# Feed-forward half of an encoder block: weight blocks of the next quarter prepared inside the present one, seven products in a new order, squares on ScalarE

## The chip, the core and the metric

The program runs on one core of a Trainium2 chip. Five engines work side by side, each through its own list of instructions in a fixed order: TensorE (PE; its weight loads are PEld) multiplies matrices and writes PSUM banks, VectorE (DVE) and ScalarE (ACT) do elementwise work, GpSimd (POOL) does a little of it, and SyncE (SP) issues most of the transfers. An instruction that waits holds up everything behind it on its own engine. The metric is the device time of one execution in microseconds (us). The kernel before takes 742.55 us (median of three runs, 742.44 to 743.73).

## The reference, cut to what matters

One encoder layer on 512 rows of 1024 columns, in float32. The change lies in the second half, and in the weights that are loaded for it:

```python
x = layer_norm(DEEPNORM_ALPHA * x + mix, ln1_g[l], ln1_b[l])         # x: 512 x 1024
h = jnp.square(jax.nn.relu(jnp.einsum("bsd,df->bsf", x, w_ff1[l])))   # w_ff1: 1024 x 4096
ff = jnp.einsum("bsf,fd->bsd", h, w_ff2[l])                          # w_ff2: 4096 x 1024
x = layer_norm(DEEPNORM_ALPHA * x + ff, ln2_g[l], ln2_b[l])
```

`mix` comes from two attention branches, two branch products with sigmoid gates, and an output product.

## The kernel before, in words

**Precision.** Every float32 operand is split into a high part h, rounded by a copy on ACT (L84), and a low part l = source - h, made on DVE (L85). A product is three matmuls: h*h, h*l and l*h (L184 to L186 where the weights are stationary, L189 to L191 where the activations are). A *split* below is this pair, one instruction on ACT and one on DVE.

**The feed-forward half in four quarters.** Each quarter takes 1024 of the 4096 hidden columns. Its first part is four *column pairs* (`t_pair`): each multiplies all 1024 rows of `w_ff1` for two blocks of 128 hidden columns, 8 steps of 3 matmuls for each of two banks, 48 matmuls; four pairs are 192. The two results of a pair go to the functions `first(i)` and `second(i)`: ReLU on ACT (L896), the square on DVE (L897), and then sums, differences and splits. These are the left operands of Strassen's scheme in Winograd's form: the quarter's second product, a 2 by 2 block product, is done with **seven products** instead of eight. Their left operands are A11, A12, A22 and the sums S1 to S4 of blocks of h; their right operands are four blocks of `w_ff2` (b11, b12, b22, b21 for each i from 0 to 3) and sums of these. Product n is 2 banks by 4 values of i by 3 matmuls: 24 matmuls, and seven are 168. `prepare(n, i)` makes the right operand of product n for block i: the subtractions that it needs (L866) and a split. `run(n, ...)` issues product n's matmuls. Before, the order is 1, 6, 2, 7, 5, 4, 3; A11, S2 and S3 are the left operands of 1, 6 and 7.

**Where the weights come from.** SP loads `w_ff1` as 512 KB chunks (`raw`, L126), which are split into `wh` and `wl` ahead of their use, and `w_ff2` as 256 KB blocks (L927). Before, a quarter's sixteen blocks lie in the tiles called X; they are loaded and split while the quarter's own column pairs run and while its products run.

**Results.** A product's two banks are added into U (`u`) and into the residual rows x1 (`x`) on DVE (L853, L855, L1018, L1025); only then is the bank free for the next product but one. Two pairs of banks, W and Z, collect products 7 and 5 over all four quarters. In the last quarter the rows are finished one block of 128 at a time: layer norm (statistics on DVE at L863, L728; L736 and L742 apply it) and the store. The last block is cut in two halves of 256 columns that share one bank.

**What sets the order.** The order of the instructions on each engine is fixed when the program is built. A scheduler interleaves the program's text with what it takes to be ready; tiles are handed out again in the order in which they come free. The V tiles (24 of them) hold right and left operands in a round: a split into a V tile waits until the product that read its earlier content has gone by on PE.

**Before the feed-forward half** come the second branch product (L610 on DVE, L613 on POOL, L615 on ACT, L616 on DVE), and the output product in two halves of columns with four row blocks each: L719 adds, L723 to L790 do the first layer norm, and L801 turns the normalised rows on PE. The sixteen gates lie in the tiles called G, which come free one by one during the second branch product; in the feed-forward half of the kernel before, G holds A12 with A22, and S4 with S1.

Of the kernel before, what the change touches and what calls it, by code (L numbers as in the profile page):

```python
# [40 lines left out]
def block_kernel(ctx, tc, w, w2, x_t, x, pos, relb, bgate, lq1, lk1, lq2, lk2, subg,  # L41
# [773 lines left out]

    c0 = next_chunk[0] + 4
    for i in range(4):
        dest[c0 + i] = ([vt(), vt()], [vt(), vt()])
    for n, _ in enumerate(s_group(mh, ml, evac_res(0))):
        prefetch(c0 + 5, min(c0 + 4, next_chunk[0] + 3))  # L820
    fin = evac_res(1)
# [19 lines left out]

    U = [late.tile([P, S], F32, name=f"u{b}") for b in range(2)]
    touched = set()

# [8 lines left out]
    def row_stats(s, nh, lo=0, hi=S):  # L858
        width = S if s < NT - 1 else 256
# [4 lines left out]

    def sub(out, a, b):
        V.tensor_tensor(out=out, in0=a, in1=b, op=ALU.subtract)  # L866

    LEFT = {1: "A11", 2: "A12", 3: "S4", 4: "A22", 5: "S1", 6: "S2", 7: "S3"}
    lo_rows, hi_rows = slice(0, 256), slice(256, S)

    class Quarter:


        def __init__(self, q):
            self.q = q
            self.ops = {n: [None] * 4 for n in range(1, 8)}
            self.raw = [None] * 4
            self.a = {}
            a11 = self.halves(vt)
            self.ops[1] = [(vt(), vt()) for _ in range(4)]  # L880
            s2 = self.halves(vt)
            self.ops[6] = [(vt(), vt()) for _ in range(4)]
            s3 = self.halves(lambda: late.tile([P, S], FR, tag="s3", bufs=4, name=name("s3")))
            for i in range(4):
                self.a["A11", i], self.a["S2", i], self.a["S3", i] = a11[i], s2[i], s3[i]

        def halves(self, make):

            two = [(make(), make()) for _ in range(2)]
            return [tuple(t[:, 256 * j:256 * (j + 1)] for t in pair)  # L890
                    for pair in two for j in range(2)]


        def square(self, ps):
            t = tmp_tile()
            A.activation(t, ps, AF.Relu)  # L896
            V.tensor_tensor(out=t, in0=t, in1=t, op=ALU.mult)  # L897
            return t

        def first(self, i):  # L900
            def f(ps):
                t = self.t0 = self.square(ps)
                sub(t[:, hi_rows], t[:, lo_rows], t[:, hi_rows])
                split(t[:, lo_rows], *self.a["A11", i])
                split(t[:, hi_rows], *self.a["S3", i])
            return f

        def second(self, i):
            def f(ps):
                t, t0 = self.square(ps), self.t0  # L910
                s2 = tmp_tile()[:, lo_rows]
                sub(s2, t[:, hi_rows], t0[:, hi_rows])
                for left, right in (("A12", "A22"), ("S4", "S1")):
                    h, l = gt(FR), gt(FR)
                    split(t, h, l)
                    self.a[left, i] = h[:, lo_rows], l[:, lo_rows]
                    self.a[right, i] = h[:, hi_rows], l[:, hi_rows]
                    if left == "A12":
                        split(s2, *self.a["S2", i])
                        sub(t[:, lo_rows], t[:, lo_rows], s2)  # L920
                        V.tensor_tensor(out=t[:, hi_rows], in0=s2, in1=t0[:, lo_rows], op=ALU.add)
            return f


        def load(self, i, r, c, t=None):
            t = t or xt()
            nc.sync.dma_start(out=t, in_=w2[self.q, i, r, :, c * S:(c + 1) * S])  # L927
            return t

# [3 lines left out]
        def prepare(self, n, i, parts=None):  # L933
            b11, b12, b22, b21 = self.raw[i]
            src = {1: b11, 6: b22, 2: b21, 7: b12, 5: b11, 4: b22, 3: b11}[n]
            if n == 6:
                sub(b22, b22, b11)
# [221 lines left out]
```

## Time and profile before

| what | us |
|---|---|
| median of three runs (lowest, highest) | 742.55 (742.44, 743.73) |
| the profiled execution, its own time | 744.0 |
| its span from first to last instruction | 742.2 |
| PE busy | 709.8 |
| DVE busy | 546.9 |
| ACT busy | 361.9 |

The span is what the traces show; the execution's own time holds 1.8 us beside it. Times in the rows are us from the start of the span. In 40 equal slices the page gives PE nine tenths or more nearly everywhere; slices with less lie at the last fifth of the run, and DVE is at nine there in its turn.

### The profile page before, as it was taken

What the parts mean: (1) busy time and instruction counts of PE and PEld (TensorE: products, weight loads), DVE (VectorE), ACT (ScalarE), POOL (GpSimd) and SP (SyncE); (2) the same over time, 40 slices, a digit from 0 to 9 for tenths busy, and PEclk for the clock granted to TensorE, in tenths of its full rate; (3) what the DMA queues carried; (4) which work ended last, traced back from release to release, by engine and by line L of the source; (5) the groups of instructions that cost most, each with busy time, mean ns of one, the idle gap of its engine ahead of it and who ended that gap; (6) DMA issues with size and microseconds to landing.
All of it is one profiled execution on the core that took longest, in us unless ns stands there. A gap on an engine that the chain in (4) does not pass through costs nothing.

```text
span 742.2 us, 9457 instructions
## 1 busy us (share of the span) xinstructions
PE 709.8 (96%) x3259; PEld 583.1 (79%) x3259; DVE 546.9 (74%) x1046; ACT 361.9 (49%) x666; POOL 100.5 (14%) x107
## 2 busy tenths in 40 slices
PE   9999999999999999999999879999999989999991
PEld 7888888888888888888898658887688868888771
DVE  6567578765678656747779996389946798288998
ACT  5556566545567665325455461256514563155420
POOL 1022367631111210141000000000000000000001
PEclk9999999999999999999999989999999999999996
DMA  8554224232322122614272328021451308111013
GB/s 301 181 165 127 73 81 120 69 114 86 115 85 86 57 86 86 218 66 170 78 254 94 114 67 275 31 83 57 150 191 57 113 1 283 58 58 57 1 60 110
DMA packets 34511, 83.07 MB, mean 112 GB/s; under 512 B 5408, under 2 KB 6176, under 8 KB 34464
## 3 DMA queue, kind: packets, MB, share of 16 engines
q1 hardware_dynamic: 33600, 81.37, 33.4%
q10 hardware_dynamic: 864, 1.11, 0.4%
q8 instruction: 25, 0.41, 0.2%
q14 instruction: 22, 0.18, 0.1%
HBM read 75.65 MB, written 2.10 MB: 105 GB/s over the span
## 4 chain that ended last, share of the span: by engine, by line
PE 73%; DVE 20%; ACT 4%; issue 2%; DMA 1%; DVEq 0%; ACTq 0%
PE mm L184 9%; PE mm L186 9%; PE mm L185 9%; DVE V L85 5%; PE st L184 4%; PE st L185 4%; PE st L186 4%; PE mm L190 4%; PE mm L191 4%; PE mm L189 4%; DVE X L866 3%; PE st L190 2%; PE st L191 2%; PE st L189 2%; DVE G L85 1%
## 5 line engine op out<-in xcount | busy, mean ns | idle before, releaser
L85 DVE TENSOR_TENSOR wl<-raw,wh 128x1024 fp32r<-128x1024 f32 (+1 forms) x86 | 105.0, 1221 | 27.1 <-ACT wh L84 27.1
L84 ACT CAST wh<-raw 128x1024 fp32r<-128x1024 f32 (+1 forms) x86 | 88.6, 1030 | 69.1 <-PE mm L185 25.1
L184 PE MATMUL mm<-X,wh 128*128 128x512 f32 x256 | 103.2, 403 | 0.0
L186 PE MATMUL mm<-X,wl 128*128 128x512 f32 x256 | 99.9, 390 | 0.0
L185 PE MATMUL mm<-X,wh 128*128 128x512 f32 x256 | 99.8, 390 | 0.0
L84 ACT CAST V<-X 128x512 fp32r<-128x512 f32 x108 | 61.6, 618 | 40.3 <-DMA X<-in_w_dram 25.1
L186 PE MATMUL st<-x1t,wl 128*128 128x512 f32 (+1 forms) x200 | 76.1, 381 | 0.0
L185 PE MATMUL st<-x1t,wh 128*128 128x512 f32 (+1 forms) x200 | 76.1, 381 | 0.0
L184 PE MATMUL st<-x1t,wh 128*128 128x512 f32 (+1 forms) x200 | 75.9, 381 | 0.0
L85 DVE TENSOR_TENSOR V<-X,V 128x512 fp32r<-128x512 f32 x108 | 70.9, 680 | 5.0 <-ACT V L84 5.0
L186 PEld LDWEIGHTS mm<-X,wl 128*128 128x128 f32 x256 | 48.0, 188 | 10.5
L184 PEld LDWEIGHTS mm<-X,wh 128*128 128x128 f32 x256 | 48.2, 188 | 8.8
L185 PEld LDWEIGHTS mm<-X,wh 128*128 128x128 f32 x256 | 48.2, 188 | 8.6
L767 POOL TENSOR_SCALAR s<-s 128x1 f32<-128x1 f32 x1 | 0.4, 410 | 398.3 <-DVE s L751 398.3
L285 ACT ACTIVATE e<-e,s 128x128 f32<-128x128 f32 (+3 forms) x64 | 36.0, 563 | 35.4 <-DVE s L283 34.7
L378 POOL TENSOR_SCALAR e<-e,s 128x128 f32<-128x128 f32 (+3 forms) x32 | 36.8, 1149 | 66.3 <-DVE s L287 62.4
L186 PEld LDWEIGHTS st<-x1t,wl 128*128 128x128 f32 x200 | 37.6, 188 | 7.6 <-DVE wl L85 0.5
L185 PEld LDWEIGHTS st<-x1t,wh 128*128 128x128 f32 x200 | 37.6, 188 | 7.2
L184 PEld LDWEIGHTS st<-x1t,wh 128*128 128x128 f32 x200 | 37.5, 188 | 7.0
L866 DVE TENSOR_TENSOR X<-X,X 128x512 f32<-128x512 f32 x64 | 42.3, 680 | 0.1
L189 PE MATMUL mm<-wh,X 128*128 128x512 f32 x96 | 39.0, 409 | 0.7 <-ACT wh L84 0.7
L190 PE MATMUL mm<-wl,X 128*128 128x512 f32 x96 | 38.4, 400 | 0.0
(267 smaller groups left out, 1600.0 us busy)
## 6 DMA issues: line engine op xcount, KB each, us to landing
raw<-in_w_dram SPq DMA_DIRECT2D x86, 512.0 KB
X<-in_w_dram SPq DMA_DIRECT2D x80, 256.0 KB
q<-q SPq DMA_DIRECT2D x32, 128.0 KB
G<-in_relb_dram SPq DMA_DIRECT2D x8, 256.0 KB
x<-in_x_dram SPq DMA_DIRECT2D x4, 512.0 KB
e<-in_x_t_dram SPq DMA_DIRECT2D x7, 256.0 KB
raw<-in_w_dram SPq DMA_DIRECT2D x4, 256.0 KB
out_dram<-x SPq DMA_DIRECT2D x3, 256.0 KB
```

The source lines that it names most:

```text
L84: A.copy(out=h, in_=src)
L85: i = (eng or V).tensor_tensor(out=l, in0=src, in1=h.bitcast(F32), op=ALU.subtract)
L184: T.matmul(ps, lw_h, rh, start=first, stop=False)
L185: T.matmul(ps, lw_h, rl, start=False, stop=False)
L186: T.matmul(ps, lw_l, rh, start=False, stop=last)
L189: T.matmul(ps, ah, w_h, start=first, stop=False)
L190: T.matmul(ps, ah, w_l, start=False, stop=False)
L191: T.matmul(ps, al, w_h, start=False, stop=last)
L285: A.activation(e[:, :n], e[:, :n], AF.Exp, bias=nm, scale=-1.0, accum_out=sums)
L378: G.tensor_scalar(ex[:, :n], ex[:, :n], r, None, op0=ALU.mult)
L767: G.tensor_scalar(nmr, mv[:, 0:1], -1.0, None, op0=ALU.mult)
L866: V.tensor_tensor(out=out, in0=a, in1=b, op=ALU.subtract)
```

## The change

Five things, all in the feed-forward half and just ahead of it.

1. The class `Quarter` loads its sixteen blocks of `w_ff2` when it is made, into G tiles in place of X tiles, and it is made during the **quarter before** (ahead of product 4); the first one during the first half of the output product. The three sums of the right operands are a function of their own, `sums(i)`, and with product 7's operand they are made then too.
2. The products run in the order **7, 5, 1, 6, 2, 4, 3**; product 5's operand is prepared within the column pairs, the others one product ahead.
3. Two blocks are loaded a second time, since sums overwrite them (in `prepare`, at n = 7 and n = 5; before, one block).
4. The square moves from DVE to ACT.
5. In the last quarter, the residual rows are finished in the order 2, 0, 3, 1 with products 4, 2 and 3 for each block; the last block is row block 1 (`LAST_ROW`), where it was 3. Operands A12/A22 and S4/S2 lie in X tiles, S3 and S1 in V tiles, A11 in a pool of its own.

```diff
+        def __init__(self, q):
...
+            self.raw = [[self.load(i, r, c) for r, c in ((0, 0), (0, 1), (1, 1), (1, 0))]
+                        for i in range(4)]
+            self.ops[7] = [(vt(), vt()) for _ in range(4)]
...
         def square(self, ps):
             t = tmp_tile()
             A.activation(t, ps, AF.Relu)
-            V.tensor_tensor(out=t, in0=t, in1=t, op=ALU.mult)
+            A.activation(t, t, AF.Square)
             return t
...
+        def sums(self, i):
+            b11, b12, b22, b21 = self.raw[i]
+            sub(b11, b12, b11)
+            sub(b12, b22, b12)
+            sub(b22, b22, b11)
...
+            src = {1: b12, 2: b21, 3: b11, 4: b22, 5: b11, 6: b22, 7: b12}[n]
             self.ops[n][i] = self.ops[n][i] or parts or (vt(), vt())
             split(src, *self.ops[n][i])
-            if n == 1:
-                sub(b11, b12, b11)
-                sub(b12, b22, b12)
+            if n == 7:
+                self.load(i, 0, 0, b12)
             if n == 5:
                 self.load(i, 1, 1, b11)
+            if n == 6:
+                sub(b22, b21, b22)
...
     for n, _ in enumerate(s_group(mh, ml, evac_res(0))):
         prefetch(c0 + 5, min(c0 + 4, next_chunk[0] + 3))
+        if n == 0:
+            qt = Quarter(0)
+        if n in (2, 4):
+            for i in (n - 2, n - 1):
+                qt.sums(i)
+                qt.prepare(7, i)
...
     for q in range(4):
-        qt, last = Quarter(q), q == 3
+        last = q == 3
+        qt.left_tiles()
+        qt.ops[5] = [(vt(), vt()) for _ in range(4)]
...
-            for n, k in ((), ((1, 0),), ((1, 1), (6, 0)), ((1, 2), (1, 3), (6, 1)))[i]:
-                qt.prepare(n, k)
+            prepare(5, (i,))
...
+        qt.run(7, W, **ends)
+        prepare(1)
...
+        qt.run(5, Z, **ends)
+        prepare(6)
...
+        prepare(2)
         X = bank_pair()
         qt.run(1, X)
-        prepare(6, (2, 3))
...
+        prepare(4)
         X = bank_pair()
         qt.run(6, X)
-        prepare(7)
...
         if not last:
-            qt.run(7, W, **ends)
-            prepare(4)
-            qt.run(5, Z, **ends)
             prepare(3)
+            X = bank_pair()
+            qt.run(2, X)
+            following = Quarter(q + 1)
+            for b in range(2):
+                add_to(b, 0, X[b])
+            for i in range(4):
+                following.sums(i)
+                following.prepare(7, i)
             X = bank_pair()
             qt.run(4, X)
...
         for b in range(2):
+            X, Y, X2 = ([mm_bank()] * 2 for _ in range(3))
...
+            qt.run(4, X, (b,))
...
+            qt.run(2, Y, (b,))
...
+            for lo, hi in ((0, 256), (256, S)) if b == LAST_ROW else ((0, S),):
+                qt.run(3, X2, (b,), cuts=((lo, hi),))
+                add_to(b, 1, X2[b][:, lo:hi], lo, hi)
+                row_stats(b, 1, lo, hi)
+            (layer_norm_last if b == LAST_ROW else layer_norm)(b, *lnc, store_row(b))
```

PE, early in the second quarter's products, the kernel before: product 6 for both row blocks (banks o_5099 and st_5100), with its waits; the first name behind the arrow is the weight part, the second the left operand.

```order
2328 L191 MATMUL st_5100<-V_4637,V_4634 128x512
2329 L189 MATMUL o_5099<-V_4639,V_4633 128x512 [waits Activation_49]
2330 L189 MATMUL st_5100<-V_4639,V_4633 128x512
2331 L190 MATMUL o_5099<-V_4640,V_4633 128x512 [waits DVE_49]
2332 L191 MATMUL o_5099<-V_4639,V_4634 128x512
2333 L189 MATMUL o_5099<-V_4641,V_4635 128x512 [waits Activation_49]
2334 L190 MATMUL st_5100<-V_4640,V_4633 128x512
```

The same engine and quarter, the kernel after: the second product that runs is now 5, into bank mm_4341 and then mm_4342.

```order
2329 L189 MATMUL mm_4341<-V_4705,V_4695 128x512
2330 L190 MATMUL mm_4341<-V_4706,V_4695 128x512
2331 L191 MATMUL mm_4341<-V_4705,V_4696 128x512
2332 L189 MATMUL mm_4341<-V_4707,V_4695 128x512 [waits Activation_49]
2333 L190 MATMUL mm_4341<-V_4708,V_4695 128x512
2334 L191 MATMUL mm_4341<-V_4707,V_4696 128x512 [waits DVE_49]
2335 L189 MATMUL mm_4342<-V_4701,V_4693 128x512
```

Before, each i of the second product waits for ACT and for DVE to prepare its weights. After, the only wait there is for the fourth block's left operand S1 (V_4695 and V_4696).

DVE in the second quarter's products, the kernel before, at the splits for products 2, 7 and 5 (V from X) between additions into u and x.

```order
746 L85 TENSOR_TENSOR V_5084<-X_4655,V_5083 128x512 [waits Activation_49]
747 L1025 TENSOR_TENSOR u_3817<-u_3817,o_5099 128x512 [waits PE_49]
748 L85 TENSOR_TENSOR V_5088<-X_4742,V_5087 128x512 [waits Activation_49]
749 L1025 TENSOR_TENSOR u_3818<-u_3818,st_5100 128x512 [waits DVE_49,PE_49]
750 L85 TENSOR_TENSOR V_5092<-X_4750,V_5091 128x512 [waits Activation_49]
```

The kernel after at the matching place: splits for product 6, its subtractions, and subtractions for the third quarter's blocks (G_5277 to G_5281).

```order
730 L85 TENSOR_TENSOR V_5131<-G_4571,V_5130 128x512 [waits Activation_49]
731 L823 TENSOR_TENSOR G_5277<-G_5279,G_5277 128x512 [waits DMAHW3_49,DMAHW2_49]
732 L823 TENSOR_TENSOR G_4571<-G_4573,G_4571 128x512 [waits DMAHW1_49,DVE_49]
733 L85 TENSOR_TENSOR V_5136<-G_4579,V_5135 128x512 [waits PE_49,Activation_49]
734 L823 TENSOR_TENSOR G_5279<-G_5281,G_5279 128x512 [waits DMAHW4_49,DVE_49]
735 L823 TENSOR_TENSOR G_4579<-G_4581,G_4579 128x512 [waits DVE_49]
736 L85 TENSOR_TENSOR V_5141<-G_4587,V_5140 128x512 [waits Activation_49]
737 L823 TENSOR_TENSOR G_5281<-G_5281,G_5277 128x512 [waits DVE_49]
```

DVE now waits there for transfers of the next quarter (DMAHW) and, through ACT, for PE to free V tiles.

DVE in the second branch product, the difference between the two kernels (+ is new): G_3459 to G_3471 are blocks of the first quarter's `w_ff2`.

```order
+L823 TENSOR_TENSOR G_3459<-G_3461,G_3459 128x512
+L823 TENSOR_TENSOR G_3461<-G_3463,G_3461 128x512
 L616 SCALAR_TENSOR_TENSOR X_3335<-G_2528,X_3334 128x512
+L823 TENSOR_TENSOR G_3463<-G_3463,G_3459 128x512
 L610 SCALAR_TENSOR_TENSOR G_2790<-G_2790,st_3338 128x512
 L85 TENSOR_TENSOR wl_3424<-raw_3357,wh_3423 128x1024
+L823 TENSOR_TENSOR G_3467<-G_3469,G_3467 128x512
 L616 SCALAR_TENSOR_TENSOR X_3354<-G_2722,X_3353 128x512
 L610 SCALAR_TENSOR_TENSOR G_2937<-G_2937,st_3363 128x512
```

Twelve such subtractions and four splits (product 7's operand) now stand in DVE's queue between the branch product's additions and the output product's first layer norm.

## Rows read from the trace of the kernel before

**Rows 1.** Who waited for whom on PE, whole span: us, times, longest

```profile
PE st L189 <- DVE x L853: 10.4, 4, 7.9
PE o L190 <- DVE V L85: 7.0, 5, 5.3
```

**Rows 2.** Busy time by stretch: us, PE, PEld, DVE, ACT, POOL (count), PEclk, DMA

```profile
418.96:468.00 49.04, 41.80 (x170) 32.38 (x168) 39.29 (x66) 19.07 (x34) 0.00 (x0) 0.93 0.46 150
511.52:553.87 42.35, 40.29 (x169) 31.05 (x168) 33.28 (x56) 16.29 (x29) 0.00 (x0) 1.00 0.44 149
597.39:639.72 42.33, 40.28 (x170) 31.08 (x168) 33.26 (x56) 16.30 (x29) 0.00 (x0) 1.00 0.44 150
683.24:733.55 50.31, 41.43 (x181) 33.00 (x179) 50.18 (x92) 15.66 (x30) 0.00 (x0) 0.93 0.17 56
...
468.00:511.52 43.52, 43.52 (x194) 36.04 (x192) 30.93 (x53) 21.06 (x36) 0.00 (x0) 1.00 0.22 73
```

**Rows 3.** PE in order of time, first quarter's products: start, us, operation, [idle before]

```profile
423.27 0.39 PE L191 MATMUL st<-V,V 128*128 128x512 f32 x1
428.97 0.80 PE L190 MATMUL o<-V,V 128*128 128x512 f32 x1 [5.31 <-DVE V L85]
...
433.52 0.39 PE L189 MATMUL st<-V,V 128*128 128x512 f32 x1
```

**Rows 4.** PE in order of time, second quarter's products

```profile
525.80 0.50 PE L189 MATMUL st<-V,G 128*128 128x512 f32 x1 [0.97 <-DVE x L853]
```

**Rows 5.** DVE groups, 468 to 553.9: count, busy us, mean ns, idle before

```profile
L866 DVE TENSOR_TENSOR X<-X,X 128x512 f32<-128x512 f32 x16 | 10.6, 680 | 0.0
...
L897 DVE TENSOR_TENSOR lt<-lt 128x512 f32<-128x512 f32 x8 | 5.5, 684 | 5.4 <-ACT lt L896 5.4
```

**Rows 6.** ACT groups, whole span

```profile
L896 ACT ACTIVATE lt<-st 128x512 f32<-128x512 f32 x24 | 14.2, 592 | 35.8 <-PE st L186 35.6
...
L527 ACT ACTIVATE e<-o 128x512 f32<-128x512 f32 x4 | 2.3, 585 | 1.0 <-PE o L524 1.0
```

**Rows 7.** DVE in order of time, 425 to 560

```profile
447.94 5.50 DVE L85 TENSOR_TENSOR V<-X,V 128x512 fp32r<-128x512 f32 x9
...
483.40 0.42 DVE L866 TENSOR_TENSOR lt<-lt,lt 128x256 f32<-128x256 f32 x1
483.73 0.42 DVE L921 TENSOR_TENSOR lt<-lt,lt 128x256 f32<-128x256 f32 x1
```

**Rows 8.** All engines in order of time, end of the last quarter

```profile
730.09 0.20 DVE L728 BATCH_NORM_AGGREGATE s<-bn 128x2 f32<-128x12 f32 x1
730.21 0.37 DVE L853 TENSOR_TENSOR x<-x,st 128x256 f32<-128x256 f32 x1
...
730.63 0.58 PE L189 MATMUL st<-V,G 128*128 128x256 f32 x1 [7.91 <-DVE x L853]
...
734.19 0.40 DVE L853 TENSOR_TENSOR x<-x,st 128x256 f32<-128x256 f32 x1
```

**Rows 9.** The chain that ended last, in order of time: start, us, what

```profile
359.71 0.87 PE mm L801 x8
...
707.55 3.13 DMA X<-in_w_dram
...
731.24 0.07 DVE s L741
731.31 0.65 DVE x L736
```

**Rows 10.** DVE in order of time, output product and first layer norm

```profile
330.33 0.69 DVE L616 SCALAR_TENSOR_TENSOR X<-G,X 128x512 fp32r<-128x512 f32 x1 [1.85 <-ACT X L615]
...
348.00 0.68 DVE L719 SCALAR_TENSOR_TENSOR x<-x,mm 128x512 f32<-128x512 f32 x1
...
354.31 0.69 DVE L719 SCALAR_TENSOR_TENSOR x<-x,o 128x512 f32<-128x512 f32 x1 [0.96 <-PE o L191]
```

**Rows 11.** ACT in order of time, first layer norm's end

```profile
356.78 0.82 ACT L789 ACTIVATE lt<-x,ln,ln 128x512 f32<-128x512 f32 x1 [0.48 <-DVE ln L787]
```

More of the change, by code (lines that the diff above doesn't have):

```diff
@@ L863, in row_stats @@
             V.bn_stats(out=stats[s][:, c // width, :], in_=x1[s][:, c:c + width])
[L865 to L896, printed above, removed]
-            V.tensor_tensor(out=t, in0=t, in1=t, op=ALU.mult)
[L898 to L928, printed above, removed]
-        def loads(self, i):
-            self.raw[i] = [self.load(i, r, c) for r, c in ((0, 0), (0, 1), (1, 1), (1, 0))]
[L933 to L937, printed above, removed]
-            self.ops[n][i] = self.ops[n][i] or parts or (vt(), vt())
-            split(src, *self.ops[n][i])
-            if n == 1:
-                sub(b11, b12, b11)
-                sub(b12, b22, b12)
-            if n == 6:
-                sub(b22, b21, b22)
-            if n == 5:
-                self.load(i, 1, 1, b11)
-        def run(self, n, ps, blocks=(0, 1), first=True, stop=True, cuts=((0, S),)):
-            jobs = [(b, lo, hi) for b in blocks for lo, hi in cuts]
-            order = [(j, i) for i in range(4) for j in jobs] if n == 1 else                 [(j, i) for j in jobs for i in range(4)]
-            for (b, lo, hi), i in order:
-                ah, al = (t[:, b * P:(b + 1) * P] for t in self.a[LEFT[n], i])
-                wh, wl = (t[:, lo:hi] for t in self.ops[n][i])
-                smm(ps[b][:, lo:hi], ah, al, wh, wl, first and i == 0, stop and i == 3)
@@ L981, in block_kernel, with prepare @@
     for q in range(4):
-        qt, last = Quarter(q), q == 3
+        last = q == 3
+        qt.left_tiles()
+        qt.ops[5] = [(vt(), vt()) for _ in range(4)]
+        def prepare(n, which=range(4), parts=None):
+            for i in which:
+                qt.prepare(n, i, parts and [t[:, i, :] for t in parts])
         for i in range(4):
-            for n in ((0,), (1, 2), (3,), ())[i] if q else (i,):
-                qt.loads(n)
             evacs = [qt.first(i), qt.second(i)]
@@ L992, in block_kernel @@
             if q == 0 and i in (1, 2):
-                for s in (2, 3) if i == 1 else (0, 1):
+                for s in (0, 1) if i == 1 else (2, 3):
                     affine(s, *norm.pop(s), *lnc1)
-            for n, k in ((), ((1, 0),), ((1, 1), (6, 0)), ((1, 2), (1, 3), (6, 1)))[i]:
-                qt.prepare(n, k)
-        def prepare(n, which=range(4), parts=None):
-            for i in which:
-                qt.prepare(n, i, parts and [t[:, i, :] for t in parts])
+            prepare(5, (i,))
         if last:
```

123 lines of the change are left out of this document (79 added, 44 removed).

## The prediction

> **What bounds the kernel now.** I read the page first: PE is busy nearly throughout, so the time is PE's work plus PE's waits. Then PE's waits by releaser [rows 1]. Two of them stand out, and both lie in the changed part: for a DVE addition that must free a bank (10.4 us, 7.9 in one piece), and for a DVE split of a V tile (7.0 us, 5.3 in one piece). Then the stretches [rows 2]. The last row there is a quarter's column pairs: 192 matmuls in 43.52 us, 0.2267 us each, with no loss. At that pace a quarter's 168 product matmuls take 38.08 us. The four product stretches take 49.04, 42.35, 42.33 and 50.31 us. They lose 10.96, 4.27, 4.25 and 12.23 us, together 31.7.
>
> The reader is to see three kinds of loss. In the first quarter PE stands for 5.31 us at 428.97, for a DVE split, and comes back at half pace; the stretch shows a granted clock of 0.93 against 1.00 beside it, that is, some of it at 1.2 instead of 2.4 GHz [rows 2, 3]. In the middle quarters the clock stays at 1.00 and PE waits in small pieces, the longest 0.97 us for a bank [rows 4]. In the last quarter DVE is busy 50.18 of 50.31 us [rows 2]: it is the bound there. PE waits 7.91 us for the shared bank before the second half of the last product, needs 2.92 us for 12 narrow matmuls, to 733.55, and the last addition starts at 734.19 [rows 2, 8]. From there to the span's end, 742.2, there are 8.01 us.
>
> **Durations.** Between starts DVE takes 0.60 us for 128x512: nine in 5.50 us, of which the last shows 0.08 more than its pitch; 0.33 for 128x256 (483.40 to 483.73) [rows 7]; about 0.65 for a row operation of the last layer norm, 0.07 for a reciprocal [rows 9] and 0.12 for an aggregate [rows 8].
>
> **The square.** Eight squares per quarter leave DVE: 8 x 0.60 = 4.8 us. Before, DVE stood 5.4 us in 85 us ahead of them for ACT's ReLU [rows 5]. On ACT a Square of this size took 585 ns and the ReLU takes 592 [rows 6], the square on DVE 684 [rows 5]. So the chain from bank to left operand is some 0.1 us shorter. ACT has room: 21.06 of 43.52 us busy in the pairs, 16.29 of 42.35 in the products [rows 2]. I take 0 for it on PE's path; what it gives is DVE time.
>
> ScalarE and VectorE differ here by 99 ns in ScalarE's favour. [...]
>
> **Ahead of the feed-forward half.** DVE gets 12 subtractions and 4 splits before the first layer norm: 16 x 0.60 = 9.6 us. Its queue has holes there, 1.85 us before 330.33 and 0.96 before 354.31 [rows 10]. Walked through with those holes filled, the addition of 348.00 moves to about 352. The four additions and statistics behind it then end near 356.6, so the addition of 354.31 starts near 356.6, 2.3 us late. Before, the chain from that start to ACT's normalised half (end 357.60) takes 3.29 us [rows 10, 11]; after, it ends at 359.9. PE wants it at 359.71, behind products that it does anyway [rows 9]. Cost: 0.2 us. Bounds: 0, if DVE's holes hold more, and 5, if a load is late: DVE then waits at the head of its queue and everything behind it. A 256 KB load took 3.13 us [rows 9]; the loads go out on SP as gates free G tiles, from about 313, over ten us ahead of their use. So I take the low end.
>
> **First quarter.** Sixteen blocks' sums and product 7's operand are done before the pairs begin. What remains for DVE in the pairs is per pair 5.8 us, and 13 for the normalised rows and product 5's last splits, 36 in all for 43.5. No backlog is carried into the products, where before it held PE for 5.31 us. Product 7 finds its operands; S1 of the last block, needed second-last in product 5, is ready about T+5.8 against T+7.5 (T: start of a quarter's first product, here 418.96). Product 5's weights were split in the pairs; the tightest later split, for the last block of product 2, is at 439.6 against 442.8. So nothing waits, the clock stays up, and the stretch falls to 38.08: minus 10.96. Bounds: minus 6 (the gap goes, the clock still drops) and minus 10.96.
>
> **Middle quarters.** The last left operands now wait for V tiles, which free as PE passes through product 7: ACT's casts stand at T+1.4 to T+6.2, the high part of S1 is at T+6.5 and the low part at T+7.2 against T+7.5 and T+7.9. This is the narrow place. Behind it DVE's queue, at 0.60 us each, ends the splits for product 6 at T+14.0 against T+18.4, those for product 2 at T+19.4 against T+21.8, the additions for the first x1 bank at T+20 against T+21.8, product 4's at T+24.2 against T+27.2, product 3's at T+29.0 against T+32.6. DVE's work there is 54 x 0.60 + 4 x 0.33 = 33.7 us, as before 33.28 of 42.35 [rows 2], now in 38.08. The new wait on transfers: the next quarter's blocks go into tiles freed at T+4.5 and later, and land, by 3.13 us each, two to four us ahead of their subtractions. DVE's splits and PE's additions are queued behind these subtractions, so a late block would reach PE. I take minus 4.27 and minus 4.25; bounds are 0 and these.
>
> **Last quarter.** DVE stays the bound. From the first split after T to the first cut addition I count 59 operations of 128x512 (35.4 us), 4 of 128x256 (1.3), 12 of the layer norm's (7.8) and six small ones (0.6): 45.1, where before it took 46.97 (683.24 to 730.21) [rows 2, 8]. After the addition PE follows in 0.42 us (730.63), and needs the same 2.92. The last addition comes 0.05 later; before 0.64, since DVE had statistics in front of it. Then 8.01. That is T+56.5 in place of T+58.96: minus 2.4. Bounds: minus 4 (PE's order leaves DVE's last operations shorter) and plus 2 (DVE, whose order is fixed, waits once for PE at a row's end).
>
> **Sum.** 0.2 - 10.96 - 4.27 - 4.25 - 2.4 = -21.7. The profiled execution took 744.0 (span 742.2 and 1.8 outside), so 722.3; the median of the runs is 1.45 lower, which gives 720.9. I put 721.2, since each of four hand-overs between pairs and products may keep 0.1.
>
> **Rivals.**
> DVE falls behind in the middle products. For: it has 34 us of work in 38, waits on V tiles and transfers now stand in its queue, and each quarter's 32 hand-overs from ACT may cost 0.1 us (an estimate after the 0.08 that a DVE instruction shows beyond its pitch [rows 7]). Against: before, it had the same work and its backlog fed PE late by only 4.3 us in the quarter. 32 x 0.1 is 3.2 us a quarter, where the queue has next to no slack at the narrow place; over three quarters some 9 us are not regained: 730.
>
> The early preparation clogs the first layer norm. For: 9.6 us of additional queue on DVE between additions that free PE's banks. Against: holes and 2.1 us of slack in front of the transposes. At the bound of 5 plus 1 for the half pace that follows a gap as at 428.97: 727.
>
> The blocks don't come early. That "load in the quarter before" may not be what happens: the G tiles of a quarter's blocks are free only when that quarter's last splits have read them. If the loads follow the splits of products 4 and 3, the second, third and fourth quarter start with weights late, as they do now; only the first quarter gains, 10.96, less 0.2, and something of the last: 731. Against: the walk above frees them from T+4.5.
>
> Slower than before: the narrow place gives way. ACT's casts of the last left operands are queued behind casts that wait for V tiles, and PE frees these only by going on; product 5 stands until S1 is there. Today's slack is 0.3 to 0.7 us. If S1 were 5.3 us late, as the split at 428.97 was, and PE came back at half pace as it did there to 433.52, a quarter would lose about 8: four quarters would eat the 21.7 and leave some 10 on top, 753. It decides from about 5.4 us lost per quarter. Against: ACT is busy under half of the time.
>
> **How the numbers follow.** Forecast 60%, own range 719.5 to 724. DVE behind (730): 14%. Clogged layer norm (727): 10%. Blocks not early (731): 8%. Slower (753): 4%. No change, where gains and losses cancel: 4%, split between the sides. The range 719 to 730 holds the forecast nearly whole, the clogged layer norm and half of DVE behind. What a measurement can't tell from no change is 0.2%, 1.5 us. Faster 94%, same 2%, slower 4%.
>
> **What would show it.** Right: product stretches of about 38.1 us in the first three quarters at a clock of 1.00; no PE wait over 1 us but that before the last cut, which stays at several us; transposes beginning near 359.9; the addition of 354.31 at about 356.6; DVE at some 34 of 38 us in the middle products; 56.5 us from the last T to the end. Wrong: a PE wait for a V split inside product 5 or 7 (the narrow place), PE waits for banks in products 1 to 4 with DVE full (behind), DVE idle with a transfer as its releaser (blocks late), or a clock under 1.00 in a middle quarter.

## The result, and the profile after

| | before | after |
|---|---|---|
| median (lowest, highest), four runs each, us | 742.91 (742.44, 743.73) | 724.20 (723.29, 725.08) |
| the profiled execution: time, span, us | 744.0, 742.2 | 725.1, 721.9 |

The ratio is 0.9747 (95% interval 0.973 to 0.9764), 18.7 us off. Forecast were 721.2, with 719.5 to 724 as the forecast's own range and 719 to 730 as the whole one. Below, ratios are to runs of the kernel before that were taken together with the run, and one slow execution of e1, at a granted clock of 0.655, is left out everywhere.

PE's waits over the whole span, the two longest of the kernel after (columns as in [rows 1]):

```profile
PE st L189 <- DVE x L951: 7.9, 1, 7.9
PE mm L801 <- issue: 2.0, 1, 2.0
```

The waits for V splits of [rows 1] are gone, and so are the bank waits but one: that before the last cut (711.25). The second row is new. It lies ahead of the feed-forward half, at the first layer norm's transposes; "issue" says only that the profile shows no releaser. The next section shows what PE stood for there.

Busy time by stretch, the kernel after (columns as in [rows 2]): the first quarter's products, the second's column pairs, then three product stretches.

```profile
420.81:459.07 38.26, 38.26 (x169) 31.54 (x168) 38.17 (x64) 17.98 (x32) 0.00 (x0) 1.00 0.53 167
459.07:502.59 43.52, 43.52 (x193) 36.04 (x192) 25.66 (x42) 25.14 (x43) 0.00 (x0) 1.00 0.32 102
502.59:540.86 38.27, 38.27 (x170) 31.54 (x168) 34.70 (x58) 17.53 (x30) 0.00 (x0) 1.00 0.51 165
584.38:622.64 38.26, 38.26 (x169) 31.54 (x168) 34.70 (x58) 17.51 (x30) 0.00 (x0) 1.00 0.51 166
666.16:714.22 48.06, 40.08 (x181) 33.31 (x179) 45.43 (x84) 12.71 (x24) 0.00 (x0) 0.94 0.13 47
```

The first three product stretches are PE's work alone at a clock of 1.00: 38.26 for 49.04, 38.27 for 42.35, 38.26 for 42.33 [rows 2]. In the first of them DVE is busy 38.17 of 38.26 us: nothing is late, and nothing is left over. In the last quarter DVE is still the bound:

```profile
710.78 0.41 DVE L951 TENSOR_TENSOR x<-x,st 128x256 f32<-128x256 f32 x1
711.25 0.58 PE L189 MATMUL st<-x1t,X 128*128 128x256 f32 x1 [7.95 <-DVE x L951]
714.22 0.42 DVE L951 TENSOR_TENSOR x<-x,st 128x256 f32<-128x256 f32 x1 [2.56 <-PE st L191]
```

These are all engines in order of time at the end, beside [rows 8]. The first cut addition comes 44.6 us after the quarter's first product (46.97 before), PE again needs 2.9 us at half pace, and from the last addition to the span's end it is 7.7 (8.01 before).

To compare what lies ahead of the quarters, a fixed point is needed, since the first 50 us of an execution differ from run to run. The first transpose of the attention part (L294) serves: PE groups by line, number, ns (least, median, most), first and last start. The kernel before:

```profile
L294 PE MATMUL st<-ident,e x80: 270/272/303, 51.3 to 164.2; 128*128 128x128 f32 x80
L801 PE MATMUL mm<-ident,lt x32: 270/272/328, 359.6 to 377.7; 128*128 128x128 f32 x32
```

The kernel after:

```profile
L294 PE MATMUL st<-ident,e x80: 270/272/303, 50.4 to 163.4; 128*128 128x128 f32 x80
L801 PE MATMUL mm<-ident,lt x32: 270/273/332, 361.7 to 379.9; 128*128 128x128 f32 x32
```

The layer norm's transposes begin 311.3 us after that point, 308.3 before: 3.0 late. The quarters' first product begins 370.41 after it (420.81 - 50.4), 367.66 before (418.96 - 51.3): 2.75 late. So the span's 20.3 us are made up as 0.9 (earlier start, chance) - 2.75 + 10.78 + 4.08 + 4.07 + 3.22 (last quarter to the end: 58.96 to 55.74); the column pairs take 43.52 in both.

### The profile page after: what moved, and what is told of

It is laid out like the page before. It is cut to its first block, busy times and chain, and to the rows that moved or that the text cites. A ratio compares the mean times of both kernels' runs of the same rounds, so it can differ in the third digit from the quotient of the medians.

```text
span 721.9 us, 9483 instructions
## 1 busy us (share of the span) xinstructions
PE 700.4 (97%) x3259; PEld 583.0 (81%) x3259; DVE 535.1 (74%) x1014; ACT 382.1 (53%) x698; POOL 101.3 (14%) x107
## 4 chain that ended last, share of the span: by engine, by line
PE 84%; DVE 9%; ACT 2%; POOL 2%; issue 2%; DMA 0%; DVEq 0%
PE mm L184 9%; PE mm L186 9%; PE mm L185 9%; PE st L185 6%; PE st L184 6%; PE st L186 6%; PE st L189 4%; PE st L191 4%; PE st L190 4%; PE mm L189 4%; PE mm L190 4%; PE mm L191 4%; PE o L184 2%; POOL G L613 2%; PE o L185 2%; PE o L186 2%
## 5 line engine op out<-in xcount | busy, mean ns | idle before, releaser
L84 ACT CAST V<-G 128x512 fp32r<-128x512 f32 x108 | 63.7, 619 | 50.7 <-DVE G L823 25.3
L85 DVE TENSOR_TENSOR V<-G,V 128x512 fp32r<-128x512 f32 x108 | 73.8, 684 | 1.4 <-ACT V L84 1.4
L823 DVE TENSOR_TENSOR G<-G,G 128x512 f32<-128x512 f32 x64 | 46.1, 731 | 0.1
L191 PE MATMUL st<-V,X 128*128 128x512 f32 x116 | 45.0, 389 | 0.0
L190 PE MATMUL st<-V,X 128*128 128x512 f32 x116 | 44.9, 389 | 0.0
L189 PE MATMUL st<-V,X 128*128 128x512 f32 x116 | 44.8, 391 | 0.0
L185 PEld LDWEIGHTS st<-x1t,wh 128*128 128x128 f32 x200 | 37.6, 188 | 7.1
```

The lines of the kernel that those rows point to most:

```text
L84: A.copy(out=h, in_=src)
L85: i = (eng or V).tensor_tensor(out=l, in0=src, in1=h.bitcast(F32), op=ALU.subtract)
L185: T.matmul(ps, lw_h, rl, start=False, stop=False)
L189: T.matmul(ps, ah, w_h, start=first, stop=False)
L190: T.matmul(ps, ah, w_l, start=False, stop=False)
L191: T.matmul(ps, al, w_h, start=False, stop=last)
```

## What held the first layer norm

PE stands twice here where it did not in the kernel before: 0.62 us for the low part of a weight chunk, and 1.96 us ahead of the transposes. Together they are 2.58 of the 2.75 us. In the kernel after:

```profile
343.39 0.50 PE L190 MATMUL mm<-wl,X 128*128 128x512 f32 x1 [0.62 <-DVE wl L85]
...
361.75 1.07 PE L801 MATMUL mm<-ident,lt 128*128 128x128 f32 x8 [1.96 <-issue]
```

**DVE and POOL lengthen each other.** DVE in order of time, second branch product and output product, the kernel after:

```profile
323.08 2.39 DVE L823 TENSOR_TENSOR G<-G,G 128x512 f32<-128x512 f32 x2
...
328.56 1.78 DVE L823 TENSOR_TENSOR G<-G,G 128x512 f32<-128x512 f32 x1
...
336.57 1.78 DVE L85 TENSOR_TENSOR V<-raw,V 128x512 fp32r<-128x512 f32 x1
...
352.50 0.69 DVE L85 TENSOR_TENSOR V<-raw,V 128x512 fp32r<-128x512 f32 x1 [2.37 <-ACT V L84]
353.11 0.68 DVE L719 SCALAR_TENSOR_TENSOR x<-x,mm 128x512 f32<-128x512 f32 x1
```

POOL in order of time, the same place:

```profile
323.24 1.68 POOL L613 TENSOR_TENSOR G<-G,G 128x512 f32<-128x512 f32 x1 [2.06 <-DVE G L610]
327.58 2.20 POOL L613 TENSOR_TENSOR G<-G,G 128x512 f32<-128x512 f32 x1 [2.67 <-DVE G L610]
...
335.60 2.20 POOL L613 TENSOR_TENSOR G<-G,G 128x512 f32<-128x512 f32 x1 [2.07 <-DVE G L610]
```

A subtraction that takes 0.68 elsewhere takes 1.78 where POOL's gate product runs beside it, or two take 2.39 in place of 1.28. There are four such places, 1.1 us each, 4.4 in all: three hold added subtractions (the third a pair at 331.69, 2.39), the fourth is the split of 336.57, which was there before. The twelve subtractions average 939 ns:

```profile
L823 DVE TENSOR_TENSOR G<-G,G 128x512 f32<-128x512 f32 x12 | 11.3, 939 | 0.1
```

So the "holes" of DVE [rows 10] were not free: POOL works in them. The Trainium skill (SBUF — State Buffer, SBUF: two separate sides) says that VectorE with two SBUF inputs and a GpSimd instruction that reads SBUF take one port pair in turn, whole instruction by whole instruction, and that the loser blocks. The trace agrees: POOL's product of 323.24 ends at 324.92, and the second subtraction of the pair ends at 325.47, 0.55 us later.

**What PE waits for at the transposes.** ACT in order of time, the kernel after, then e5 (an experiment below in which product 7's four splits stand behind the layer norm):

```profile
347.50 1.66 ACT L84 CAST V<-raw 128x512 fp32r<-128x512 f32 x3
350.90 1.05 ACT L84 CAST wh<-raw 128x1024 fp32r<-128x1024 f32 x1 [1.74 <-DMA raw<-in_w_dram]
351.86 0.61 ACT L84 CAST V<-raw 128x512 fp32r<-128x512 f32 x1
```

```profile
347.07 1.14 ACT L84 CAST V<-raw 128x512 fp32r<-128x512 f32 x2 [3.40 <-DMA raw<-in_w_dram]
348.98 1.06 ACT L84 CAST wh<-raw 128x1024 fp32r<-128x1024 f32 x1 [0.77 <-DMA raw<-in_w_dram]
```

In the kernel after, the last V cast (351.86) stands on ACT behind the cast of the next weight chunk, which waits 1.74 us for its transfer. Its own data were there: it is the second half of a chunk whose first half was cast in the group of 347.50. So DVE's split of 352.50 waits 2.37 us at the head of its queue, and behind it the four additions and the layer norm. In e5 both halves are cast before the next chunk; DVE waits 1.30 us for them, and PE does not stand at the transposes.

Seven traces, that of the change and six of experiments whose edits come later, have the same instructions in the same order on every engine up to there. Only how long ACT waits for the chunk differs, by chance. PE's wait follows DVE's, 0.4 us shorter in each:

| us | change | e2 | e3 | e6 | e7 | e9 | e10 |
|---|---|---|---|---|---|---|---|
| DVE waits for the last V cast | 2.37 | 2.43 | 1.32 | 1.54 | 1.68 | 2.66 | 2.32 |
| PE waits ahead of the transposes | 1.96 | 2.04 | 0.92 | 1.10 | 1.28 | 2.21 | 1.93 |

The awaited chunk is the one that SP issues at 345.17, 0.03 us after the DVE split that frees its tile (the one of 344.46). So DVE's queue set the issue, and not the loads ahead of it on SP. Whether other transfers beside it lengthened its way is open.

## The experiments

**e1, half of it later.** Sums and product 7's splits of two of the first quarter's four blocks moved behind the layer norm.

```diff
-        if n in (2, 4):
+        if n == 2:
...
+            if q == 0 and i < 2:
+                qt.sums(i + 2)
+                qt.prepare(7, i + 2)
             prepare(5, (i,))
```

> The changed kernel, with the sums and product 7's splits of the last two blocks of the first quarter moved from the output product into the first two column pairs. Theory (DVE's queue held the first layer norm, the transposes came 2.0 us late): the transposes go back to about 359.8, the first quarter's products start 1.8 us earlier, and since DVE has 9 us idle in these pairs nothing is lost behind: 722.4 against 724.2. Rival (a late 512 KB weight load held the queue, whatever stands in it): the transposes stay at 361.7 and the time at 724.2. Second rival: the first quarter's products now wait for their splits: 726 or more.

Measured: 722.06, 722.16 and 723.89 us; ratio 0.9721 (0.9704 to 0.9737). The interval touches that of the change, so the time alone doesn't separate them. The stages, read from e11 (the same edit), do: the first quarter's first product comes 368.2 us after the fixed point, against 370.41 in the change and 367.66 before, and PE does not stand at the transposes. The theory holds as far as it says that what stands in the queues ahead of the layer norm held it. What moved, though, are two splits alone, with their casts on ACT and two loads behind them; e5 shows why.

**e5, all of it later, as far as the text goes.**

```diff
-        if n in (2, 4):
-            for i in (n - 2, n - 1):
-                qt.sums(i)
-                qt.prepare(7, i)
...
+            if q == 0:
+                qt.sums(i)
+                qt.prepare(7, i)
             prepare(5, (i,))
```

> The changed kernel with none of the first quarter's sums and product 7's splits ahead of the first layer norm: all sixteen stand in its column pairs; the loads stay early. Theory (DVE's queue ahead of the layer norm cost 2.75 us, and DVE's 9 idle us in the first quarter's pairs take 9.6 us nearly whole): the four additions of the output product's first half go back to 348 to 350, the transposes to where they were before, and the products of the first quarter start up to 2.7 us earlier but may wait about 1 us for a split: 721.5 to 723 against 724.2. Rival (the pairs have no room, as in the kernel before): a gap of some us in the first quarter's products with half clock behind it, 726 to 730.

Measured: 722.81; 0.973 (0.9711 to 0.9749). But the edit did not do what that text says. The scheduler put all twelve subtractions back where they had been; only the four splits moved, with their casts on ACT and the four loads that refill b12 behind them. DVE groups ahead of the layer norm (310 to 349) in e5:

```profile
L823 DVE TENSOR_TENSOR G<-G,G 128x512 f32<-128x512 f32 x12 | 11.1, 940 | 0.1
```

This brings 2.06 us at the first product (418.15 - 49.8 = 368.35 after the fixed point): the wait at the transposes is gone. What is left to the kernel before, 0.69, is the other wait, for the low part of the weight chunk, which is 0.74 here. So in this order the subtractions, with all their meetings with POOL, cost the first product no more than 0.7. The first quarter's products give 0.74 back (39.00 for 38.26), as DVE has no time to spare there. Taking the subtractions away as well was not tried, and neither was moving splits, casts and refills one at a time.

**e9, the refills later.** The four loads that refill b12 issued behind the output product.

```diff
-            if n == 7:
+            if n == 7 and self.q:
                 self.load(i, 0, 0, b12)
...
+    for i in range(4):
+        qt.load(i, 0, 0, qt.raw[i][1])
```

> The changed kernel, with the sums and splits of the first quarter where it has them, but the four loads that refill their blocks (b12, after product 7's split) issued behind the output product in place of inside its first half. Theory (SP stands at these loads until DVE has split, and the weight chunks of the output product's second half stand behind it: the last chunk is issued at 349.56, DVE waits 2.37 us for it at the head of its queue): the chunk is issued some us earlier, that wait goes and the four additions start 2 to 3 us earlier; the transposes begin 1 to 2 us earlier: 722.2 to 723.2 against 724.2. Rival (the number of DVE instructions ahead of the layer norm is what counts): DVE is full until 351 anyway and the time stays within 0.5 of 724.2.

Measured: 723.23; 0.9735 (0.9721 to 0.975). The edit did not do what the text says: the scheduler put the four loads back. SP in order of time, the change, then e9, both 295.1 us after the fixed point:

```profile
345.54 3.14 SPq L881 DMA_DIRECT2D G<-in_w_dram  x3
```

```profile
344.19 3.14 SPq L881 DMA_DIRECT2D G<-in_w_dram  x3
```

Instruction for instruction, PE, ACT and SP do the same in both traces, so e9 is the change once more and tests neither theory. (Its text also takes the chunk issued at 349.56 for the awaited one; that is the chunk of 345.17.) As a second trace of the change it shows the spread: the transposes begin 311.6 us after the fixed point (360.7 - 49.1) for 311.3, and the time is 1.0 lower.

**e4, the square alone, on the kernel before.**

```diff
             A.activation(t, ps, AF.Relu)
-            V.tensor_tensor(out=t, in0=t, in1=t, op=ALU.mult)
+            A.activation(t, t, AF.Square)
```

> The kernel before with the square on ACT, that alone. Theory (the first quarter's backlog is DVE's overload in its pairs, about 6 us): 4.8 us less DVE work takes away most of the 5.31 us gap and, with it, the half clock after it: the first quarter's products fall from 49.0 to 39 to 42; the last quarter gains 1 to 2; together 732 to 736 against 742.9. Rival (the gap comes from the order in which splits and products are prepared): under 2 us, 741 to 743.

Measured: 734.65 against 743.72; 0.988 (0.9866 to 0.9895). Nearly half of the change's gain from one of its five parts. Stretches of e4: the first quarter's products, then the second's.

```profile
416.60:463.00 46.40, 41.16 (x170) 32.21 (x169) 36.62 (x61) 18.77 (x33) 0.00 (x0) 0.96 0.48 159
506.51:546.91 40.40, 39.52 (x169) 31.27 (x168) 31.37 (x52) 16.08 (x28) 0.00 (x0) 1.00 0.47 157
```

The first gains 2.64, each middle one 1.9, the last quarter 1.4, together 7.9; the rest of the 9.1 is an earlier start of its profiled execution or chance. The total is inside the theory's 732 to 736, but not by its reason: it put the gain into the first quarter, at 39 to 42 us. There the wait for a V split is halved, not gone:

```profile
423.95 0.79 PE L190 MATMUL o<-V,V 128*128 128x512 f32 x1 [2.66 <-DVE V L85]
```

**e2, the change without the square.** The same two lines, the other way round.

> The changed kernel with the square back on DVE, that alone. Theory (the square gave DVE time where DVE had time to spare anyway): the column pairs and the first three product stretches keep their times within 0.5 us each, the last quarter loses about 1, since one or two squares of its last pair stand in front of DVE's queue: 725 to 726. Rival (DVE's 4.8 us per quarter is what the gain rests on): S1 of the last block comes 0.7 us or more too late, PE waits in product 5 and loses 2 to 5 us in each quarter: 732 to 744.

Measured: 727.19; 0.9786 (0.9771 to 0.9801), 3.0 slower than the change, between the theory and the rival. Stretches of e2 (first and second quarter's products), and PE at the first one's end:

```profile
420.17:461.06 40.89, 39.07 (x169) 31.22 (x167) 39.69 (x68) 17.47 (x32) 0.00 (x0) 1.00 0.50 159
504.72:543.14 38.42, 38.42 (x170) 31.48 (x168) 35.52 (x60) 17.12 (x29) 0.00 (x0) 1.00 0.51 167
```

```profile
461.06 0.50 PE L184 MATMUL st<-x1t,wh 128*128 128x512 f32 x1 [1.56 <-DVE x L953]
```

The middle quarters lose 0.15 each, the last 0.6. The first loses 2.6: there DVE was full. So by these stages the square is worth 7.9 us by itself and 3.5 on top of the rest (by the medians 9.1 and 3.0). The parts pay for one and the same thing, DVE's time, and their gains must not be added.

**e3, each quarter's blocks in its own quarter.** Loads, sums and product 7's splits of quarters two to four not in the quarter before, but in their own column pairs.

```diff
-            following = Quarter(q + 1)
...
-            for i in range(4):
-                following.sums(i)
-                following.prepare(7, i)
...
+        if q:
+            qt = Quarter(q)
         qt.left_tiles()
...
+            if q:
+                qt.sums(i)
+                qt.prepare(7, i)
             prepare(5, (i,))
```

> The changed kernel, with the blocks of the second, third and fourth quarter loaded at the start of their own quarter and their sums and product 7's splits made in its column pairs (as the first quarter's are made ahead). Theory (what counts is that DVE's work is done before the products that need it; the pairs have 18 us of idle DVE in 43.7): the product stretches stay at 38.0, 723 to 725. Rival (the early load and preparation is what removes the middle quarters' waits): each of three quarters loses about 4 again: 734 to 737.

Measured: 725.77; 0.9761 (0.9741 to 0.9781). Stretches of e3: the second and third quarter's products.

```profile
501.69:539.95 38.26, 38.26 (x169) 31.57 (x168) 33.01 (x55) 15.03 (x26) 0.00 (x0) 1.00 0.46 146
583.47:621.74 38.27, 38.27 (x170) 31.56 (x168) 33.06 (x55) 15.03 (x26) 0.00 (x0) 1.00 0.46 147
```

The theory holds: in the middle quarters, loading a quarter early brings nothing that the column pairs' idle DVE doesn't. The time lies 0.8 above its 723 to 725, since it costs 2.1 us in the last quarter (57.84 to the end), where DVE now stands at its start for splits of product 3's operand:

```profile
665.29 1.90 DVE L85 TENSOR_TENSOR x1t<-G,x1t 128x512 fp32r<-128x512 f32 x3 [1.68 <-ACT x1t L84]
668.85 0.69 DVE L85 TENSOR_TENSOR x1t<-G,x1t 128x512 fp32r<-128x512 f32 x1 [1.67 <-ACT x1t L84]
```

**e7, products 1 and 5 exchanged:** 7, 1, 5, 6, 2, 4, 3.

```diff
-        qt.run(5, Z, **ends)
-        prepare(6)
...
         X = bank_pair()
         qt.run(1, X)
+        prepare(6)
+        qt.run(5, Z, **ends)
```

> The changed kernel with products 5 and 1 in exchanged places: 7, 1, 5, 6, 2, 4, 3. Theory (the order gives the weights that are split last the time that product 5, split within the pairs, takes on PE): product 1's weights are cast at 2.7 to 6.2 us after the first product begins, PE wants them at 5.4, and its first additions wait for DVE; PE loses 1 to 3 us in each of four quarters, in the first ones with some half clock: 728 to 738. Rival (DVE has enough slack for any order, the preparation ahead is what counts): 723.5 to 725.5.

Measured: 724.49; 0.975 (0.9735 to 0.9764). The rival holds for these two products: the middle quarters stay at 38.27, the first loses 0.6 (38.88). Stretches of e7:

```profile
420.49:459.37 38.88, 38.75 (x169) 31.38 (x168) 38.27 (x64) 18.38 (x32) 0.00 (x0) 1.00 0.52 167
502.89:541.16 38.27, 38.27 (x169) 31.54 (x168) 34.70 (x58) 17.51 (x30) 0.00 (x0) 1.00 0.51 166
```

**e6, U's six additions of the last quarter on POOL.**

```diff
-                add_to(s, nh, U[b])
+                y = x1[s][:, nh * S:(nh + 1) * S]
+                G.tensor_tensor(out=y, in0=y, in1=U[b], op=ALU.add)
```

> The changed kernel with the six additions of U into the residual rows of the last quarter on POOL in place of DVE. Theory (DVE bounds the last quarter: 45.4 of 48.0 us busy, PE waits 7.9 us for it): 6 x 0.60 = 3.6 us leave DVE and the time falls by 2 to 3.6, to 721 to 722; PE's last wait shortens by as much. Rival (the last quarter is bound by the chain through PE and the row operations, or POOL's slower additions hold DVE at the statistics behind them): no gain or up to 2 us slower, 724 to 726.

Measured: 722.11; 0.9726 (0.9704 to 0.9747). In its own stage it gained next to nothing: from the quarter's first product to the last addition 47.74 us (664.25 to 711.99) against 48.06. DVE and POOL in e6 in order of time:

```profile
687.54 6.16 POOL L1070 TENSOR_TENSOR x<-x,u 128x512 f32<-128x512 f32 x4 [350.85 <-DVE u L1043]
...
688.45 1.19 DVE L85 TENSOR_TENSOR V<-G,V 128x512 fp32r<-128x512 f32 x1
690.82 0.69 DVE L961 BATCH_NORM_STATS2 bn<-x 128x6 f32<-128x512 f32 x1 [1.19 <-POOL x L1070]
691.43 1.13 DVE L85 TENSOR_TENSOR V<-G,V 128x512 fp32r<-128x512 f32 x1
693.38 0.69 DVE L951 TENSOR_TENSOR x<-x,st 128x512 f32<-128x512 f32 x1 [0.82 <-PE st L191]
```

3.6 us left DVE; 1.19 and 0.82 came back as waits, and 0.5 each as the longer splits at 688.45 and 691.43. The statistics need POOL's first additions at once. The median is 2.1 below the change's, near the theory's 721 to 722, but not by its reason: beside the 0.3 of this stage the trace has 1.0 at the start and 0.9 ahead of the first product, where the edit changes nothing.

**e10, three of the six on POOL,** those of the row block that is finished last.

```diff
-                add_to(s, nh, U[b])
+                if b:
+                    y = x1[s][:, nh * S:(nh + 1) * S]
+                    G.tensor_tensor(out=y, in0=y, in1=U[b], op=ALU.add)
+                else:
+                    add_to(s, nh, U[b])
```

> The changed kernel with three of the six additions of U in the last quarter on POOL, those for the second row block of each pair, which is finished last. Theory (the last quarter is bound by DVE, and the six on POOL gained only 0.3 us in that quarter since DVE stood 1.19 us for POOL's third addition and 0.82 for PE behind it): now POOL has about 4.4 us of work and some 10 us of time, so DVE is 3 x 0.60 = 1.8 us shorter and waits for nobody; the quarter takes 53.9 in place of 55.7, the time is 722.0 to 722.7. Rival (POOL's additions lengthen the DVE instructions beside them, as two splits of 1.1 to 1.2 us in place of 0.68 show): half of it is lost, 723.2 to 724.

Measured: 718.20; 0.9665 (0.9649 to 0.9681), 6 us below the change, three times what was expected. Of these 4.2 lie in the stage: the last quarter to the span's end takes 51.57 us (55.74). The rest is an earlier start of the profiled execution (1.1) and less time outside the span. The stretch, and the first cut addition and PE behind it, in e10:

```profile
664.93:708.42 43.49, 38.84 (x181) 32.16 (x179) 43.46 (x81) 12.70 (x24) 6.47 (x3) 1.00 0.13 46
```

```profile
704.43 0.37 DVE L951 TENSOR_TENSOR x<-x,st 128x256 f32<-128x256 f32 x1
704.86 0.39 PE L189 MATMUL st<-x1t,X 128*128 128x256 f32 x1 [2.79 <-DVE x L951]
```

DVE is busy 43.46 of 43.49 us, 2.0 less than the change's 45.43, and waits for nobody. The other 2.6 of the stretch is DVE's wait of 2.56 for PE ahead of the last addition (714.22), which is gone. The order makes that so: the first cut addition now stands ahead of the previous row's normalisation, PE waits 2.8 us in place of 7.9, stays at full clock (1.00 for 0.94), and its last matmuls are done while DVE still normalises. POOL took the delay: its three additions took 6.47 us, the six of e6 8.68.

**e8, sixteen loads more, on the kernel before:** the load in `prepare` at n = 5 stands there twice.

> The kernel before with one 256 KB load of each block group issued twice: 96 loads of w_ff2 blocks as in the changed kernel, where it has 80. It tells where the time outside the span comes from: 1.8 to 1.9 us in runs of the kernel before, 2.2 us and more in runs of the changed kernel. Theory (it goes with the number of loads): the difference between time and span grows by about 0.4 us to 2.2, the span by under 1 us: 744 to 745 against 743.7. Rival (it goes with something else): the difference stays at 1.8 to 1.9.

Measured: 744.36 against 743.48 (1.0014, 1.0004 to 1.0023). Outside the span lie 1.82 to 1.93 us in its ten runs, as before. The rival holds: the number of loads alone isn't it.

**e11 and e12, both edits together:** e10 with e1, and e10 with e5.

> The changed kernel with two edits of earlier runs together: the sums and product 7's splits of the last two blocks in the first quarter's pairs, and U's three additions for the row block finished last on POOL. Theory (the two lie in different stages, the layer norm's front and the last quarter, and add up: 1.2 to 2 and 6.0): 716 to 717. Rival (the start of the first quarter's products and the last quarter share DVE's backlog, so that they overlap): 718, no better than the POOL edit alone.

> The same with all sixteen of the first quarter's sums and splits in its pairs. Theory: 1.4 us as measured for that edit alone, less 6.0: 716.5 to 717; the first quarter's products lose 0.7 us to late splits where the other keeps 38.3, so this one is up to 0.5 behind the other. Rival: 718, as above.

Measured: e11 719.03, 0.9671 (0.9658 to 0.9685); e12 717.57, 0.9659 (0.9646 to 0.9672). e12 is the fastest version here, 25.6 us below the kernel before and 6.6 below the change as measured; of it 0.6 against e10 is within the intervals. In the stages e12's two edits do add up: the first product 368.35 us after the fixed point, the last quarter 51.54 to the end; 0.76 of it goes back in the first quarter's products (39.02). e12 lies 0.6 above its 716.5 to 717, and e11, which was to be ahead of it, above both of its own (716 to 717, and 718). e11's spans are no longer than e10's (715.7 to 716.3 against 715.2 to 716.8), but it has up to 3.0 us outside the span.

## Why the prediction was right, and where it was off

**The products** came out as worked out: 38.08 was forecast for each of three stretches, 38.26 to 38.27 measured; the first quarter gave 10.78 for 10.96, the middle ones 4.08 and 4.07 for 4.27 and 4.25. The allowance of 0.1 per hand-over is about half of what is missing.

**The narrow place** is where it was put, and it held. In the second quarter ACT and DVE finish S1 of the last block at T+6.26 and T+7.09 (forecast T+6.5 and T+7.2), and PE loads it at T+7.26 and T+7.71 (T is 502.59):

```profile
508.44 0.41 ACT L84 CAST V<-lt 128x256 fp32r<-128x256 f32 x1 [1.06 <-DVE lt L873]
509.26 0.42 DVE L85 TENSOR_TENSOR V<-lt,V 128x256 fp32r<-128x256 f32 x1
510.30 0.19 PEld L191 LDWEIGHTS mm<-V,V 128*128 128x128 f32 x1
```

So 0.6 us were left, and the condition of the slower rival did not come up. No run made S1 later: e7, which puts product 5 third, gives S1 more time, and tests only whether product 1's weights, split later, come in time for the second place; in the middle quarters they do. What the prediction named as the tool, the early load, is not needed in the middle quarters (e3). These stretches take 38.3 to 38.4 with the square on DVE (38.42, e2), with late loads (38.26, e3) and in the other order (38.27, e7), and 40.40 with the square alone moved (e4). What e2, e3 and e7 share, splits and sums made ahead of the products, was not taken out by itself; that it is what removes the waits is argued, not shown.

**The square** was put at 0 on PE's path beside the rest. By the stages it is 7.9 us by itself (e4) and 3.5 on top of the rest (e2). That was hidden in the working: "36 for 43.5" in the first quarter's pairs held only with the square gone, and in the products DVE was full at 38.17 of 38.26. ACT's Square took 632 ns on the mean, a little above the 585 that it was read from and under DVE's 684:

```profile
L852 ACT ACTIVATE lt<-lt 128x512 f32<-128x512 f32 x32 | 20.2, 632 | 0.7
```

**The last quarter** gave 3.2 for 2.4: 44.6 for the 45.1 counted, and a tail shorter by 0.3. DVE as its bound is shown by e10, not by e6, where the work that left DVE came back as waits.

**Ahead of the feed-forward half** lies the term that was mis-sized: 0.2 forecast, 2.75 measured, within the bounds of 0 to 5. The step that failed is "So I take the low end": the wait at the head of DVE's queue was named as a bound and put at nothing. The walk before it was good. It put the addition of 348.00 at about 352; measured is 354.0 (353.11, and 0.9 for the earlier start), of which 2.37 are the wait. Without the wait it is 351.6, and by the table the layer norm's half would have been ready 0.4 us before PE came to it (an estimate). The load that was late was not one of the new 256 KB blocks that the prediction looked at, but an old weight chunk, and DVE met it through ACT, where a cast whose data were there stood behind it. The table of seven traces shows that this wait sets PE's; in e5, e11 and e12, where the order on ACT is another, PE does not stand at the transposes. Which of the things that these edits move together (splits on DVE, casts on ACT, refills on SP) brings the other order is open. The second part, 0.6 for a weight chunk's low part, was not in the working at all: it looked at the additions, not at the splits of the output product's weights in the same queue. POOL's row, which it did not look at either, lengthens the instructions there; how much of the 0.6 that makes was not tested.

The seven traces put the first product at 369.3 to 370.7 after the fixed point, three with the kernel before's front (before, e4, e8) at 367.2 to 367.7; so the term is 1.6 to 3.5, and the change's own trace lies in the middle. This is the clogged layer norm of the rivals at about half its price.

**Outside the span** the prediction kept 1.8 us. All runs of the kernel before show 1.8 to 1.9, those of the change 2.2 to 3.2. What sets it stays open: not the number of loads alone (e8); e10 and e12, with the same loads and another last quarter, mostly have 1.8 to 2.0.

The median is 3.0 us above the forecast, and 0.2 outside the forecast's own range. 2.5 of it are the layer norm's term, 0.4 to 1.3 the time outside the span, and 0.2 the product stretches (0.5, of which the forecast had 0.3 set aside); the last quarter took 0.8 off. The starts of the executions, which are chance, make up the rest.

## What to carry to other kernels

Where one engine's queue is short of time, parts of a change that relieve it don't add up: measure each alone and each left out. Before idle time of VectorE is filled with work, look at POOL in the same stretch, and at the order that this leaves on ScalarE: a cast behind one that waits for a transfer held VectorE for 2.37 us. And where a chain at the end is bound by one engine, take off it only the work whose result isn't wanted at once (e10 against e6).

## What the runs showed of the hardware

A 128x512 float32 addition or split on VectorE took 0.68 us, and in places 1.13 to 1.78 where a POOL instruction on SBUF operands ran beside it; POOL's took 1.28 alone and 1.68 to 2.20 beside VectorE. In e10 POOL alone paid: its three additions took 2.16 each, and VectorE's beside them stayed at 0.68 to 0.69. From one execution to the next, the first 50 us of the same instructions differed by up to 2.2 us (L294 first at 49.1 to 51.3).
